# The convolution layer's first product: three 256-column matmuls a weight tile become one of 256 and one of 512, in two banks a column pair

## The chip, the cores and the metric

The kernel runs on one core of one Trainium2 chip. The metric is the device time of one execution in microseconds (us), lower is better; the figure for a kernel is the median of its runs. The core's engines are named as in the profile: PE is TensorE (PEld its weight loads), DVE is VectorE, ACT is ScalarE, POOL is GpSimd, SP is SyncE, which here issues the DMAs.

## The reference, cut to what matters

Four layers on 256 frames of width 1024. Each layer adds a token mixer to the residual and then a squared-ReLU MLP, both behind an RMS norm. The mixers are retention, convolution, stick-breaking attention, retention. The change touches the convolution mixer of the second layer only:

```python
def conformer_conv_mixer(xn, pw1_w, pw1_b, dw_w, dw_b, ln_w, ln_b, pw2_w, pw2_b):
    h = xn @ pw1_w + pw1_b                      # (256, 1024) @ (1024, 2048)
    a, gate = jnp.split(h, 2, axis=-1)
    h = a * jax.nn.sigmoid(gate)
    h = ...   # causal depthwise convolution of h, 31 taps, + dw_b
    h = layer_norm(h, ln_w, ln_b)
    h = jax.nn.silu(h)
    return h @ pw2_w + pw2_b
```

## The kernel before, in words

**Numbers.** All weights are float32. A large product is computed from a rounded high part and a low part (the rest) of each operand, as float32r matmuls: weight high by activation high, weight high by activation low, weight low by activation high. The activations lie transposed, features on partitions: a tile `z` of 128 x 512 holds the 256 columns of the high part of 128 features and, behind them, the 256 columns of the low part.

**Weights.** They come in units of 128 x 1024 (four contraction tiles of 256 output columns), two units in one DMA into a `raw` buffer. For each unit, `unit_hi` lets ACT copy the high part into `wh` (line 354) and `unit_lo` lets DVE subtract it from the raw weights into `wl` (line 361). There are five buffers each of `wh` and `wl`.

**Two ways of a product.** `mm_b` works on one accumulator bank (`acc`, 128 x 512, four of them) that holds a column pair: 256 columns for each of the two weight tiles m. For each weight tile it issues the three matmuls of 256 columns (lines 508, 509, 510), all into the same 256 columns of the bank. `mm_w` works on two banks, one for each weight tile m: one matmul of 256 columns, weight low by activation high, into the first half of the bank (line 524), and one of 512 columns, weight high by both parts of the activation at once, into the whole bank (line 528). The two halves of a bank then still have to be added: `sum_w` lets ACT copy the second half into an SBUF tile (line 571) and DVE add the first half to it (line 572), for each of the two banks. `mm_w` with `sum_w` computes the feed-forward products of most layers; there, too, DVE multiplies the sum by the norm's factor `rb` (line 652).

**The convolution layer (`conv`).** Its first product has 16 units, n = 0 to 15: for each of four column pairs p, two units of the gate's columns (parts 0 and 1, accumulated in `pg`) and two of the value's (parts 2 and 3, in `pa`). The program order of PE and DVE is written out by hand (`manual_schedule`); ACT and POOL follow the order that the scheduler works out with a simulated timeline, and each engine works off its own queue in order. In an iteration n there come, on DVE: the low part of unit n + 3 (`fetch`), then taps of the depthwise convolution for channel tile 0 (`tap_dve`, lines 1010 and 1012), and, where a half ends, the multiplication of the product by `rb` out of the accumulator: `gate_in` (line 969) behind the gate's second unit, with the sigmoid on ACT (line 972), and `glu` (line 977) behind the value's second unit, with the two instructions of line 982 that make the gated tiles `hc` (two channel tiles a pair). For pair 0 the norm's factor is only worked out during unit 1 and broadcast during unit 2 (`norm_r`, `bcast`), so that `gate_in` of pair 0 comes behind unit 2.

The taps of channel tile 1 run beside this: ACT scales the shifted input into one of three `pr` buffers (line 1017) and POOL adds it up (line 1021), three taps an iteration.

The channel tiles 2 to 7 take their taps as matmuls of 32 x 32 blocks on PE (`taps_pe`, line 1092). For these, `spread` writes two gated tiles to DRAM (line 956) and reads them back in another layout (line 959); `pairsum` (POOL, line 992) forms sums of neighbouring columns from it. Behind the first product the order of all four engines is written out by hand: `glu(3)`, `spread(6, 1)` for the last two tiles, `pairsum(2)`, `sum_1`, `pairsum(3)`, the matmul taps of tiles 2 and 3, `shift_a`, `shift_b`, `shift_bb` (a column sum on PE, line 404, its copy on DVE, line 1154, and its broadcast on PE, line 411), the taps of tiles 4 and 5, then of 6 and 7. The accumulators for `taps_pe` come from the same four banks in rotation. Four weight loads of the second product (`unit_raw`, line 369) are issued behind the last DMA of `spread(6, 1)`.

Of the kernel before, what the change touches and what calls it, by code (L numbers as in the profile page):

```python
# [17 lines left out]
S = 256  # L18
# [224 lines left out]
def v3(ap, a, b):  # L243
    return ap.rearrange("p (a b) -> p a b", a=a, b=b)


class Trunk:
# [680 lines left out]
    def conv(self, j, nxt):  # L928
        nc = self.nc
        self.table("sigmoid_and_others")  # L930
        hc = []
        rb = None
# [3 lines left out]
        n = len(PET) * 16  # L936
# [14 lines left out]
        def spread(d0, step):  # L951
            t = self.raw.tile([P, RAWW], F32, name=self.nm("raw"), tag="raw")
            for d in range(d0, d0 + 2, step):
                rows = self.dram.tile([step, 4, 32, HL], F32, name=self.nm("hd"), tag=f"hd{step}")
                for i in range(step):
                    nc.sync.dma_start(rows[i].rearrange("j c u -> (j c) u"), hc[d + i][:, :HL])
                o, n = (d - d0) * 4 * HW, step * 4
                for s in range(4):
                    last = nc.sync.dma_start(
                        v3(t[32 * s : 32 * s + 32, o : o + n * HW], n, HW),  # L960
                        rows.rearrange("i j c u -> c (i j) u")[:, :, NG * s : NG * s + HW],
                    )
                for i in range(step):
                    h4[d + i] = t[:, o + i * 4 * HW : o + (i + 1) * 4 * HW]
            return last

        def gate_in(p, pg):
            u, sg = self.tmp(), self.tmp()
            nc.vector.tensor_mul(v3(u, 2, S), v3(pg, 2, S), self.b2(rb))
            for f in range(2):  # L970
                s = slice(f * S, (f + 1) * S)
                nc.scalar.activation(out=sg[:, s], in_=u[:, s], func=AF.Sigmoid, bias=self.p("pw1b", 8 + 2 * p + f))
            return sg

        def glu(p, pa, sg):
            va = self.tmp()
            nc.vector.tensor_mul(v3(va, 2, S), v3(pa, 2, S), self.b2(rb))
            for f in range(2):
                s = slice(f * S, (f + 1) * S)
                o = self.bigt()  # L980
                nc.gpsimd.memset(o[:, :CW], 0.0)
                nc.vector.scalar_tensor_tensor(
                    out=o[:, CW : CW + S], in0=va[:, s], scalar=self.p("pw1b", 2 * p + f), in1=sg[:, s],
                    op0=ALU.add, op1=ALU.mult,
                )
                hc.append(o)
# [40 lines left out]
        def fetch(n):  # L1027
            if n < len(pw1):
                w[n] = self.unit(("conv_pw1_w", j, "b", pw1[n][1], pw1[n][0]))
# [4 lines left out]
        def taps(n, m):  # L1034
            for k, (tap_, t, r, c) in enumerate(((tap_dve, 0, r0, n), (tap_pool, 1, r1, m))):
                for x in range(at[k], min((CW0, CW)[t], at[k] + c)):
                    tap_(t, x, r[x % 2], x < 2)
                at[k] += c
# [6 lines left out]
        with self.tc.manual_schedule(engines={mybir.EngineType.PE, mybir.EngineType.DVE}):  # L1045
            for n in range(4):
                fetch(n)
            for n in range(16):
                p, part = divmod(n, 4)
                if part == 0:  # L1050
                    pg, pa = self.acc(), self.acc()
                if p:
                    fetch(n + 3)
                    taps((2, 2, 1, 1)[part], 3)
                if n == 13:
                    spread(2, 2)
                if n == 15:
                    spread(4, 2)
                self.mm_b(
                    (pg, pa)[part // 2], w.pop(n), self.zs, part % 2 * 4, part % 2 == 0, part % 2 == 1,  # L1060
                    (lambda kk: self.norm_r(False) if kk == 3 else None) if n == 1 else None,
                )
                if n in (1, 2):
                    fetch(n + 3)
                if n == 2:
                    rb = self.bcast(self.r, "rb")
                    sg = gate_in(0, pg)
                if n == 3:
                    fetch(6)
                if part == 1 and p:  # L1070
                    sg = gate_in(p, pg)
                if part == 3 and p < 3:
                    glu(p, pa, sg)
# [152 lines left out]

        with self.tc.manual_schedule(engines=MANUAL):
            glu(3, pa, sg)
            sp = spread(6, 1)
            with self.tc.issue_after(sp.ins):  # L1230
# [314 lines left out]
```

## Time and profile before

| | |
|---|---|
| median of 3 runs | 1353.01 us (1352.46 to 1353.32) |
| the profiled execution's own time | 1354.99 us |
| its span, first to last instruction | 1353.2 us |
| PE busy | 1340.9 us, 8957 matmuls |
| DVE busy | 987.2 us, 1646 instructions |
| ACT busy | 778.2 us, 1171 instructions |
| POOL busy | 151.9 us, 139 instructions |
| mean granted TensorE clock | 0.997 |

How to read the profile's lines. In a row of the order of time stand the start, the time taken, the engine, the line of the kernel, the operation, the tile written and the tiles read, the sizes, and the count of instructions that the row merges; in brackets the idle time of the engine just before, and what released it. A row of a table of stretches has the stretch and its length, then for each engine the busy time and the count of instructions, then the granted clock as a share of full speed, the share of time in which the DMA engines were busy and what they moved in GB/s. Matmuls overlap, so that the distance between their starts tells the rate, not their durations.

### The profile page before, as it was taken

Reading aid. Unit: us, or ns where it says so; the run is one execution under the profiler, and the core shown is the slowest. Engines: PE = TensorE matmul, PEld = TensorE weight load, DVE = VectorE, ACT = ScalarE, POOL = GpSimd, SP = SyncE. Lnnn points to the kernel's source line nnn. Section 1 sums busy time; section 2 is a strip of 40 time slices with the busy share of each in tenths; the row PEclk is TensorE's granted clock in tenths of the full one; section 3 lists DMA queues with packets and bytes.
Section 4 is the critical chain, followed back from the end, with each engine's and each line's share of the span. In section 5 each row is a group of like instructions: output and inputs, shape, how many; then the busy total and the mean of one; then the engine's idle time right before and its main releaser. Section 6 shows DMA issues by size and latency. Waiting matters only on the chain.

```text
span 1353.2 us, 22237 instructions
## 1 busy us (share of the span) xinstructions
PE 1340.9 (99%) x8957; PEld 1207.9 (89%) x8957; DVE 987.2 (73%) x1646; ACT 778.2 (58%) x1171; POOL 151.9 (11%) x139
## 2 busy tenths in 40 slices
PE   9999999999999999999999999999999999999998
PEld 7989999888899898888878898888888999988886
DVE  6977778875688588765688587755697687788643
ACT  7555556774457367654568667744575555555442
POOL 3201003000169210000100010000120010100000
PEclk9999999999999999999999999999999999999999
DMA  7644445555545645555553345555554444555551
GB/s 283 214 179 152 156 156 192 207 191 188 187 157 145 198 170 204 187 186 187 186 177 126 134 159 188 194 193 196 179 177 180 156 153 160 188 186 187 203 186 62
DMA packets 39287, 240.48 MB, mean 178 GB/s; under 512 B 4368, under 2 KB 8848, under 8 KB 11792
## 3 DMA queue, kind: packets, MB, share of 16 engines
q1 hardware_dynamic: 39040, 238.80, 50.1%
q8 instruction: 70, 1.15, 0.4%
q14 instruction: 33, 0.27, 0.1%
q10 hardware_dynamic: 144, 0.26, 0.1%
HBM read 237.11 MB, written 1.93 MB: 177 GB/s over the span
## 4 chain that ended last, share of the span: by engine, by line
PE 99%; DMA 0%; ACT 0%; DVE 0%; issue 0%; SPq 0%
PE acc L528 30%; PE acc L524 16%; PE acc L508 8%; PE acc L510 8%; PE acc L509 8%; PE acc L687 6%; PE acc L923 4%; PE acc L924 4%; PE acc L925 4%; PE acc L1092 1%; PE acc L1222 1%; PE mis L404 1%; PE mis L819 1%; PE mis L843 1%; PE mis L411 0%; PE mis L1450 0%
## 5 line engine op out<-in xcount | busy, mean ns | idle before, releaser
L361 DVE TENSOR_TENSOR wl<-raw,wh 128x1024 fp32r<-128x1024 f32 (+1 forms) x440 | 547.1, 1248 | 244.0 <-ACT wh L354 237.8
L354 ACT CAST wh<-raw 128x1024 fp32r<-128x1024 f32 (+1 forms) x440 | 456.6, 1041 | 374.5 <-PE acc L528 148.8
L528 PE MATMUL acc<-z,wh 128*128 128x512 f32 x1120 | 387.4, 392 | 0.0
L524 PE MATMUL acc<-z,wl 128*128 128x256 f32 x1120 | 310.5, 281 | 0.0
L528 PEld LDWEIGHTS acc<-z,wh 128*128 128x128 f32 x1120 | 208.3, 187 | 44.6
L528 PE MATMUL acc<-big,wh 128*128 128x512 f32 x672 | 233.1, 391 | 0.0
L524 PEld LDWEIGHTS acc<-z,wl 128*128 128x128 f32 x1120 | 211.1, 189 | 1.7
L524 PE MATMUL acc<-big,wl 128*128 128x256 f32 x672 | 188.2, 280 | 0.0
L528 PEld LDWEIGHTS acc<-big,wh 128*128 128x128 f32 x672 | 125.7, 187 | 27.6
L508 PE MATMUL acc<-z,wh 128*128 128x256 f32 x512 | 145.5, 285 | 0.0
L510 PE MATMUL acc<-z,wl 128*128 128x256 f32 x512 | 145.1, 284 | 0.0
L509 PE MATMUL acc<-z,wh 128*128 128x256 f32 x512 | 144.9, 283 | 0.0
L524 PEld LDWEIGHTS acc<-big,wl 128*128 128x128 f32 x672 | 127.0, 189 | 0.0
L510 PE MATMUL acc<-big,wl 128*128 128x256 f32 x416 | 117.3, 283 | 0.0
L508 PE MATMUL acc<-big,wh 128*128 128x256 f32 x416 | 117.1, 285 | 0.0
L509 PE MATMUL acc<-big,wh 128*128 128x256 f32 x416 | 117.0, 283 | 0.0
L459 POOL TENSOR_TENSOR t<-t,t 128x512 f32<-128x512 f32 x23 | 36.0, 1566 | 682.1 <-ACT t L454 634.0
L571 ACT COPY t<-acc 128x256 f32<-128x256 f32 x164 | 57.7, 372 | 89.4 <-PE acc L528 87.1
L509 PEld LDWEIGHTS acc<-z,wh 128*128 128x128 f32 x512 | 98.1, 192 | 0.0
L508 PEld LDWEIGHTS acc<-z,wh 128*128 128x128 f32 x512 | 98.1, 192 | 0.0
L510 PEld LDWEIGHTS acc<-z,wl 128*128 128x128 f32 x512 | 98.1, 192 | 0.0
L923 PE MATMUL acc<-wh,z 128*128 128x512 f32 x224 | 87.9, 393 | 0.0
(256 smaller groups left out, 2016.0 us busy)
## 6 DMA issues: line engine op xcount, KB each, us to landing
raw<-in_w SPq DMA_DIRECT2D x214, 1024.0 KB, 4.8
raw<-in_w SPq DMA_DIRECT2D x8, 512.0 KB, 8.1
raw<-hd SPq DMA_DIRECT2D x8, 263.0 KB, 4.8
raw<-hd SPq DMA_DIRECT2D x8, 131.5 KB, 3.7
x<-in_x SPq DMA_DIRECT2D x4, 256.0 KB, 6.1
wh<-in_w SPq DMA_DIRECT2D x2, 512.0 KB, 6.1
wl<-in_w SPq DMA_DIRECT2D x2, 512.0 KB, 6.8
hd<-big SPq DMA_DIRECT2D x6, 143.5 KB, 2.3
```

Of the source, the lines that this page charges most:

```text
L354: nc.scalar.copy(hi[:, s], src[:, s])
L361: self.nc.vector.tensor_sub(lo[:, s], src[:, s], hi[:, s])
L508: nc.tensor.matmul(o, wh[:, kk, cs], ah, start=st, stop=False, **kw)
L509: nc.tensor.matmul(o, wh[:, kk, cs], al, start=False, stop=False, **kw)
L510: nc.tensor.matmul(o, wl[:, kk, cs], ah, start=False, stop=en, **kw)
L524: mm = nc.tensor.matmul(ps[m][:, :S], wl[:, kk, cs], a[:, :S], start=first and kk == 0, stop=False, **kw)
L528: nc.tensor.matmul(ps[m], wh[:, kk, cs], a, start=False, stop=last and kk == 3, **kw)
L571: nc.scalar.copy(o[:, s], ps[m][:, S:])
L687: self.tc.keep_in_program_order(nc.tensor.matmul(ps[t], l, r[:, kk], start=False, stop=kb * 2 + kk == 31 and n == 2, **kw))
L923: nc.tensor.matmul(ps[t], zh[:, s], wh[:, kk], start=k == 0, stop=False, skip_group_check=True)
L924: nc.tensor.matmul(ps[t], zh[:, s], wl[:, kk], start=False, stop=False, skip_group_check=True)
L925: nc.tensor.matmul(ps[t], zl[:, s], wh[:, kk], start=False, stop=k == 7, skip_group_check=True)
```

## The change

The gate's and the value's product each get two accumulators for a column pair instead of one, `mm_w` takes the place of `mm_b`, and `sum_w` comes ahead of the multiplication by `rb`, which then works in place on the SBUF tile of the sum. The small norm step inside unit 1 stays at the same place (the fourth contraction tile of that unit: its number is 3 within the unit for `mm_b` and 7 over the product for `mm_w`). Nothing else is edited.

```diff
         def gate_in(p, pg):
-            u, sg = self.tmp(), self.tmp()
-            nc.vector.tensor_mul(v3(u, 2, S), v3(pg, 2, S), self.b2(rb))
+            u, sg = self.sum_w(pg), self.tmp()
+            nc.vector.tensor_mul(v3(u, 2, S), v3(u, 2, S), self.b2(rb))
...
         def glu(p, pa, sg):
-            va = self.tmp()
-            nc.vector.tensor_mul(v3(va, 2, S), v3(pa, 2, S), self.b2(rb))
+            va = self.sum_w(pa)
+            nc.vector.tensor_mul(v3(va, 2, S), v3(va, 2, S), self.b2(rb))
...
                 if part == 0:
-                    pg, pa = self.acc(), self.acc()
+                    pg, pa = (self.acc(), self.acc()), (self.acc(), self.acc())
...
-                self.mm_b(
+                self.mm_w(
                     (pg, pa)[part // 2], w.pop(n), self.zs, part % 2 * 4, part % 2 == 0, part % 2 == 1,
-                    (lambda kk: self.norm_r(False) if kk == 3 else None) if n == 1 else None,
+                    before=(lambda k: self.norm_r(False) if k == 7 else None) if n == 1 else None,
                 )
```

The functions that it calls, as they stand:

```python
    def mm_w(self, ps, w, acts, k0, first, last, keep=False, before=None):
        ...
        for kk in range(4):
            if before is not None:
                before(k0 + kk)
            a = acts(k0 + kk)
            for m in range(2):
                cs = slice(m * P, (m + 1) * P)

                mm = nc.tensor.matmul(ps[m][:, :S], wl[:, kk, cs], a[:, :S], start=first and kk == 0, stop=False, **kw)
                ...
                    nc.tensor.matmul(ps[m], wh[:, kk, cs], a, start=False, stop=last and kk == 3, **kw)

    def sum_w(self, ps):
        nc = self.nc
        o = self.tmp()
        for m in range(2):
            s = slice(m * S, (m + 1) * S)
            nc.scalar.copy(o[:, s], ps[m][:, S:])
            nc.vector.tensor_add(o[:, s], ps[m][:, :S], o[:, s])
        return o
```

## The prediction

> **What bounds the kernel now.** I began with the page's busy times and the chain that ended last, and then went to the stage that the change touches: a table of busy times by stretch, and the order of time of each engine in it.
>
> ```profile
> PE 1340.9 (99%) x8957; PEld 1207.9 (89%) x8957; DVE 987.2 (73%) x1646; ACT 778.2 (58%) x1171; POOL 151.9 (11%) x139
> PE 99%; DMA 0%; ACT 0%; DVE 0%; issue 0%; SPq 0%
> ```
>
> PE (TensorE) is busy for 99% of the span and is 99% of the chain. Any PE time saved counts if nothing else then holds PE up, and any wait put on PE is paid in full, since PE has no later slack. So two questions decide: how much PE time goes, and whether the first product still keeps PE fed.
>
> ```profile
> 390.27 0.28 PE L508 MATMUL acc<-z,wh 128*128 128x256 f32 x1
> 433.95 0.28 PE L510 MATMUL acc<-z,wl 128*128 128x256 f32 x1
> 437.55 0.28 PE L510 MATMUL acc<-z,wl 128*128 128x256 f32 x1
> 349.68 0.39 PE L528 MATMUL acc<-big,wh 128*128 128x512 f32 x1
> 353.50 0.39 PE L528 MATMUL acc<-big,wh 128*128 128x512 f32 x1
> ```
>
> The first and third rows bound the first product: from 390.27 to 437.67 (one step behind the last start), 47.4 us for 16 weight units of 24 matmuls, and some small matmuls of the norm. Starts, not durations, give the rate, since matmuls overlap.
>
> Now the other engines. These three rows are the last three column pairs, p = 1, 2, 3, each from one pair's last gate multiplication to the next one's:
>
> ```profile
> 403.31:414.83 11.52, 11.52 (x98) 11.52 (x97) 10.08 (x15) 9.87 (x18) 8.25 (x8) 1.00 0.57 202
> 414.83:426.35 11.52, 11.52 (x98) 11.52 (x97) 11.26 (x14) 8.50 (x16) 11.52 (x11) 1.00 0.63 148
> 426.35:437.87 11.52, 11.52 (x100) 11.39 (x102) 7.61 (x12) 6.62 (x14) 11.52 (x15) 1.00 0.56 120
> ```
>
> The columns are length, then busy time of PE, weight loads, DVE (VectorE), ACT (ScalarE), POOL (GpSimd). In the middle pair DVE is busy for 11.26 of 11.52 us: there it is as full as PE. POOL is busy all the time, with the additions of the depthwise convolution's second tile. DVE's order is fixed by hand:
>
> ```profile
> 401.57 0.69 DVE L969 TENSOR_TENSOR t<-acc,rb 128x512 f32<-128x512 f32 x1 [1.07 <-ACT rb L417]
> 403.31 0.69 DVE L977 TENSOR_TENSOR t<-acc,rb 128x512 f32<-128x512 f32 x1
> 404.91 1.22 DVE L361 TENSOR_TENSOR wl<-raw,wh 128x1024 fp32r<-128x1024 f32 x1
> 413.10 0.48 DVE L1012 SCALAR_TENSOR_TENSOR mis<-big,prm,mis 128x256 f32<-128x256 f32 x1
> 414.83 0.69 DVE L977 TENSOR_TENSOR t<-acc,rb 128x512 f32<-128x512 f32 x1 [1.26 <-PE acc L510]
> 425.80 0.48 DVE L1012 SCALAR_TENSOR_TENSOR mis<-big,prm,mis 128x256 f32<-128x256 f32 x1
> 426.35 0.69 DVE L977 TENSOR_TENSOR t<-acc,rb 128x512 f32<-128x512 f32 x1
> 428.96 1.76 DVE L361 TENSOR_TENSOR wl<-raw,wh 128x1024 fp32r<-128x1024 f32 x1
> 437.87 0.69 DVE L977 TENSOR_TENSOR t<-acc,rb 128x512 f32<-128x512 f32 x1 [3.67 <-PE acc L510]
> 441.71 0.15 DVE L1154 COPY lns<-mis 128x2 f32<-128x2 f32 x1
> ```
>
> DVE waits for PE 1.26 us ahead of pair 1's value half, nothing ahead of pair 2's (425.80 + 0.48 runs up to 426.35), and 3.67 us ahead of pair 3's. These 4.93 us are all the room that it has.
>
> **The change part by part.**
>
> *PE.* Per weight tile three matmuls of 256 columns become one of 256 and one of 512. Old rate: ten triples between 433.95 and 437.55, 0.360 us each, so 46.1 us for 128 weight tiles; the other 1.3 us are the norm's small matmuls. New rate, from the two-bank form in the feed-forward rows (line 528): eleven pairs between 349.68 and 353.50, 0.347 us each. 128 x 0.0125 = 1.6 us, 0.10 us a unit. That is all that the change can gain here directly. The weight loads fall from three to two a tile; they run beside matmuls.
>
> The Trainium skill ("TensorE: Matmul & The Clock Gate", Part 1, "Wait — 56ns, not 53.3ns?") gives a warm matmul's start-to-start time as its columns over 2.4 GHz plus about 2.5 ns. By that, an estimate, the triple takes 327.5 ns and the pair 325.0 ns, and the gain would be 0.3 us. The rows measure 360 and 347 ns, so I keep 1.6.
>
> *ACT and DVE.* Each of the eight halves (gate and value of four pairs) gets two copies on ACT and two additions on DVE ahead of its multiplication, and the multiplication reads SBUF where it read PSUM. The same helper and the same multiplication stand in the feed-forward part:
>
> ```profile
> 367.10 0.72 ACT L571 COPY t<-acc 128x256 f32<-128x256 f32 x2 [1.37 <-PE acc L528]
> 367.50 0.77 DVE L572 TENSOR_TENSOR t<-acc,t 128x256 f32<-128x256 f32 x2 [0.52 <-ACT t L571]
> 368.31 1.50 DVE L652 TENSOR_TENSOR t<-t,rb 128x512 f32<-128x512 f32 x1
> L652 DVE TENSOR_TENSOR t<-t,rb x9: 691/692/1496, 323.9 to 945.0; 128x512 f32<-128x512 f32 x9
> L361 DVE TENSOR_TENSOR wl<-raw,wh 128x1024 fp32r<-128x1024 f32 x10 | 15.0, 1498 | 0.0
> ```
>
> The additions take 0.80 us of DVE a half (367.50 to 368.31). The multiplication from SBUF takes 0.69 us at best and 1.50 at worst. In this stage the other two-SBUF-input instruction, the low-part subtraction of line 361, averages 1.498 us (last row: the ten from 403.31 to 437.87) against 1.22 at 404.91, before POOL starts: +0.28. I take +0.27 a multiplication, between 0 and +0.80.
>
> The Trainium skill ("SBUF — State Buffer", "SBUF: two separate sides") says that a VectorE instruction with two SBUF inputs and a GpSimd one that reads SBUF exclude each other for a whole instruction. This speaks against the change. Its worst case would be about one POOL addition on each multiplication, as the 1.50 us row shows at its extreme; the +0.28 is the mean that this stage shows.
>
> The additions also wait for the copies, and ACT's order is first come, first served:
>
> ```profile
> 419.35 0.51 ACT L1017 ACTIVATE pr<-big,prm 128x256 f32<-128x256 f32 x1 [1.17 <-POOL big L1021]
> 421.94 0.68 DVE L969 TENSOR_TENSOR t<-acc,rb 128x512 f32<-128x512 f32 x1
> 425.24 0.89 ACT L972 ACTIVATE t<-t,prm 128x256 f32<-128x256 f32 x2
> ```
>
> ACT's tap scalings wait for POOL (up to 1.17 us), and what stands behind them waits too: pair 2's sigmoid ran at 425.24 though its input was ready at 422.62. A copy so placed holds up DVE, and behind it every subtraction and tap. I take 0.15 us a half, between 0 and 1.17.
>
> So a half costs DVE 0.80 + 0.27 + 0.15 = 1.22 us more. The first gate half has DVE waiting for rb (1.07 us) and costs nothing; the first value half, with POOL not yet running, 0.80. DVE's delay then runs: 0.8; pair 1's gate 2.0; the 1.26 us of room leaves 0.8, its value half 2.0; pair 2: 3.2, 4.4; pair 3's gate 5.6; the 3.67 us of room leaves 2.0; its value half 3.2. With waits and contention at nothing the last figure is +0.7, with 1.50 us multiplications and 0.5 us of waiting +8.5.
>
> *Buffers.* Each pair now takes all four accumulators, so a half must be summed before the next pair writes its banks two units (5.5 us) later: enough up to a delay of about 4 us. Late subtractions bite sooner: pair 3's last one ends at 430.72 (428.96 + 1.76), and 4.4 us later is 435.1, where the last unit wants it at about 433.3 (437.67 less 2.88, less 15 x 0.10). PE would wait some 2 us there. That costs nothing extra, because of what follows.
>
> *What waits for the last half.*
>
> ```profile
> 440.68 0.61 PE L404 MATMUL mis<-cst,big 128*128 128x1 f32 x4
> 442.23 0.71 PE L411 MATMUL mis<-cst,lns 128*128 128x128 f32 x4
> 447.58 1.06 POOL L992 TENSOR_TENSOR t<-raw 128x524 f32<-128x524 f32 x1 [1.42 <-DMA raw<-hd]
> 447.66 1.14 PE L1092 MATMUL acc<-raw,big 128*32 128x128 f32 x32
> 454.50 2.95 PE L1092 MATMUL acc<-raw,big 128*32 128x128 f32 x50 [2.03 <-issue]
> 454.50:458.00 3.50, 3.50 (x62) 3.22 (x64) 0.29 (x1) 0.31 (x1) 0.00 (x0) 0.51 0.26 48
> ```
>
> The last half's product goes to DRAM and back (spread), and tile 6's taps use it. POOL was waiting for that DMA until 447.58, and PE began those taps at 447.66: no slack. In between, PE's broadcast at 442.23 waits for DVE's copy at 441.71, behind the last half in DVE's order, with 0.4 us of slack. So PE begins tile 6 as late as the last half ends: 3.2 us less the 0.1 of slack, where without the delay it would come 1.6 us early. Nothing behind gives it back.
>
> *The sum:* +3.1 us on the profiled span of 1353.2. The profiled execution's own time is 1354.99 (1.8 around its span), 2.0 above the median of the runs, 1353.01; I add the difference to the median: 1353.0 + 3.1, rounded to 1356.0.
>
> Two more losses stand in the last two rows: 2.03 us in which PE waited for nothing that the profile shows, and then a granted clock of 0.51 for 3.5 us, so about 1.7 us lost. I leave both: the same instructions come at the same place behind the same DMAs.
>
> **The rivals.**
>
> *PE stays the bound* and the 1.6 us stand: 1351.4, not slower. For it: the room of 4.93 us, and ACT's and DVE's means of 8.33 and 9.65 of 11.52 us over the three pairs. Against it: pair 2 has no room. It decides where the delay of the last half falls under about -1.5, which even the lowest bound (+0.7) does not reach, unless the scheduler places work so that DVE's waits shrink.
>
> *The broken supply to the taps disappears:* if PE comes to tile 6 later than its DMAs do, the 2.03 us and the half clock go: 1353.0 - 1.6 - 2.0 - 1.7 = 1347.7. For it: the stall follows a crowd of DMAs. Against it: these DMAs are issued behind the same late half.
>
> *A second stretch of half clock.* If PE's new waits between 433 and 445 bring another one, it costs up to 1.7 us: 1356.0 + 1.7 = 1357.7. For it: the one in the trace follows a PE wait of 2.03 us, and my waits are as long. Against it: part of it would fall into time in which PE waits anyway.
>
> The Trainium skill ("TensorE: Matmul & The Clock Gate", "What's actually happening") says that the half clock comes after an idle window of about 3.4 us. The trace has it behind 2.03 us, so that a wait shorter than the window is no protection here.
>
> **How the numbers follow.** A time within 0.2% (2.7 us) is about what a measurement of this kernel cannot tell from no change. The DVE delay has 0.60: likeliest 1356.0, its own range 1353.7 to 1359.5; some 0.22 of it lies within 2.7 us of before, 0.38 above. PE staying the bound has 0.20, within. The second half clock has 0.13, slower. The vanished stall has 0.07, faster. Together 0.07 faster, 0.42 same, 0.51 slower. The range 1350.8 to 1360.0 leaves out the vanished stall and the tail toward +8.5.
>
> **What would show it.** In the changed trace: the first product's weight tiles at 0.347 us where PE does not wait; two copies and two additions a half, 16 of each more; the multiplications of lines 969 and 977 reading SBUF, above 0.9 us on average; DVE without an idle gap ahead of pair 1's and pair 2's value halves; PE waiting for a low part in the last unit or for a bank at the first taps; tile 6's taps starting about 3 us later than 447.66. If DVE still waits for PE ahead of pair 3's value half, the forecast is wrong toward faster; if the additions wait long for the copies, toward slower.

## The result, and the profile after

The changed kernel took 1355.76 us (median of 22 runs, 1354.42 to 1357.78) against 1353.95 us for the kernel before, timed beside it (22 runs, 1352.16 to 1354.94): a ratio of 1.0016, 95% interval 1.0010 to 1.0022. It is slower by about 2 us (1.8 by the medians, 2.2 by the ratio); forecast were 3.0, at 1356.0. That the time lies so close to 1356.0 is in part luck: the kernel before had a median 0.94 us above the 1353.01 us from which the forecast counted. The profiled execution took 1355.67 us, with a span of 1353.9 us.

The page of the kernel after, busy times and the chain that ended last:

```profile
PE 1339.2 (99%) x8829; PEld 1200.2 (89%) x8829; DVE 995.4 (74%) x1662; ACT 782.2 (58%) x1187; POOL 157.2 (12%) x139
PE 95%; DVE 2%; DMA 1%; ACT 1%; issue 0%; POOL 0%; SPq 0%; POOLq 0%; ACTq 0%
```

There are 128 matmuls fewer and 16 instructions more on each of DVE and ACT, as the change says. The chain that lay on PE for 99% of the span now lies on it for 95%. Where it leaves PE is seen in the chain in order of time (start, length, engine, tile, line), kernel after:

```profile
412.81 1.73 POOL big L1021
414.57 0.51 ACT pr L1017
415.37 0.77 DVE t L572 x2
416.16 1.03 DVE t L977
...
444.01 0.71 PE mis L411 x4
```

From the middle of the first product to the broadcast the chain runs mostly through DVE, and ahead of that through tap scalings on ACT and tap additions on POOL. PE's order of time in the kernel after, from the first product to the taps of tiles 6 and 7, with the first row of the feed-forward part last:

```profile
389.55 0.28 PE L524 MATMUL acc<-z,wl 128*128 128x256 f32 x1
...
434.34 0.39 PE L524 MATMUL acc<-z,wl 128*128 128x256 f32 x1 [1.06 <-DVE wl L361]
434.57 0.40 PE L528 MATMUL acc<-z,wh 128*128 128x512 f32 x1
...
437.00 0.39 PE L528 MATMUL acc<-z,wh 128*128 128x512 f32 x1
...
444.01 0.71 PE L411 MATMUL mis<-cst,lns 128*128 128x128 f32 x4 [1.90 <-DVE lns L1154]
444.65 4.55 PE L1092 MATMUL acc<-raw,big 128*32 128x128 f32 x96
...
450.76 1.13 PE L1092 MATMUL acc<-raw,big 128*32 128x128 f32 x32
...
456.69 1.70 PE L1092 MATMUL acc<-raw,big 128*32 128x128 f32 x50 [1.24 <-issue]
...
492.42 0.40 PE L524 MATMUL acc<-z,wl 128*128 128x256 f32 x2
```

And two rows of the same view of the kernel before:

```profile
442.87 3.01 PE L1092 MATMUL acc<-raw,big 128*32 128x128 f32 x96
491.75 0.40 PE L524 MATMUL acc<-z,wl 128*128 128x256 f32 x2
```

The two executions differ by 0.72 us already ahead of the product (390.27 against 389.55), which is not the change. So I count every start from the product's first matmul, here and in all that follows, and call four of them marks: the product's last matmul, the broadcast (line 411), the first taps of tile 6, and the feed-forward part's first matmul. Behind the last mark the two executions run equally long (about 861.4 us to the end), so it holds all that the change did.

| mark | before | after | difference |
|---|---|---|---|
| product's last matmul | 47.28 | 47.45 | +0.17 |
| broadcast | 51.96 | 54.46 | +2.50 |
| tile 6 | 57.39 | 61.21 | +3.82 |
| feed-forward | 101.48 | 102.87 | +1.39 |

PE's faster matmuls do not bring the product's end forward, since PE has to wait for DVE in the last units, 1.06 us of it in one wait for a late low part. The broadcast waits 1.90 us for DVE, and tile 6 comes 3.82 us later. Behind tile 6, 2.43 us come back, and two things give them: the wait for "issue" is 1.24 instead of 2.03 us, and the half clock has moved. Two stretches of the kernel after:

```profile
445.30:448.80 3.50, 3.50 (x78) 3.50 (x71) 3.12 (x9) 2.86 (x5) 3.27 (x5) 0.51 1.01 229
455.00:458.50 3.50, 2.26 (x75) 1.96 (x67) 1.19 (x4) 0.60 (x2) 0.00 (x0) 1.00 0.37 145
```

The granted clock is 0.51 from 445.3, ahead of tile 6, and 1.00 where it was 0.51 before. The 96 taps at 444.65 take 4.55 us for 3.01. Only about half of that seems to be lost: without a stretch at half clock (late_new, below) the changed kernel waits 0.52 us ahead of tile 6 and begins it 0.76 us earlier.

DVE's order of time in the stage, kernel after, and one row of POOL's:

```profile
403.24 0.69 DVE L977 TENSOR_TENSOR t<-t,rb 128x512 f32<-128x512 f32 x1
...
415.37 0.76 DVE L572 TENSOR_TENSOR t<-acc,t 128x256 f32<-128x256 f32 x2 [1.03 <-ACT t L571]
416.16 1.02 DVE L977 TENSOR_TENSOR t<-t,rb 128x512 f32<-128x512 f32 x1
...
430.09 0.75 DVE L977 TENSOR_TENSOR t<-t,rb 128x512 f32<-128x512 f32 x1
...
436.96 1.26 DVE L969 TENSOR_TENSOR t<-t,rb 128x512 f32<-128x512 f32 x1
...
439.46 0.76 DVE L572 TENSOR_TENSOR t<-acc,t 128x256 f32<-128x256 f32 x2 [0.31 <-ACT t L571]
440.25 1.28 DVE L977 TENSOR_TENSOR t<-t,rb 128x512 f32<-128x512 f32 x1
441.56 0.88 DVE L982 SCALAR_TENSOR_TENSOR big<-t,prm,t 128x256 f32<-128x256 f32 x2
...
443.80 0.15 DVE L1154 COPY lns<-mis 128x2 f32<-128x2 f32 x1
```

```profile
439.91 1.06 POOL L992 TENSOR_TENSOR t<-raw 128x524 f32<-128x524 f32 x1
```

DVE's waits for PE ahead of the halves (1.26 and 3.67 us) are gone. In their place stand two waits for copies. The last multiplication, 1.28 us long, began while POOL's row was running and ended 0.56 us behind that row's end. The groups of the stretch from 396 to 442 us in the kernel after (count, busy time, mean ns of one, idle time before):

```profile
L969 DVE TENSOR_TENSOR t<-t,rb 128x512 f32<-128x512 f32 x4 | 3.8, 952 | 0.3 <-ACT rb L417 0.2
L977 DVE TENSOR_TENSOR t<-t,rb 128x512 f32<-128x512 f32 x4 | 3.7, 935 | 0.1
```

### The profile page after: what moved, and what is told of

It is laid out like the page before. It is cut to its first block, busy times and chain, and to the rows that moved or that the text cites. A ratio compares the mean times of both kernels' runs of the same rounds, so it can differ in the third digit from the quotient of the medians.

```text
span 1353.9 us, 22008 instructions
## 1 busy us (share of the span) xinstructions
PE 1339.2 (99%) x8829; PEld 1200.2 (89%) x8829; DVE 995.4 (74%) x1662; ACT 782.2 (58%) x1187; POOL 157.2 (12%) x139
## 4 chain that ended last, share of the span: by engine, by line
PE 95%; DVE 2%; DMA 1%; ACT 1%; issue 0%; POOL 0%; SPq 0%; POOLq 0%; ACTq 0%
PE acc L528 31%; PE acc L524 16%; PE acc L510 7%; PE acc L508 7%; PE acc L509 7%; PE acc L687 6%; PE acc L923 4%; PE acc L924 4%; PE acc L925 4%; PE acc L1222 1%; PE acc L1092 1%; DMA raw<-in_w 1%; DVE wl L361 1%; PE mis L404 1%; PE mis L819 1%; PE mis L843 1%
## 5 line engine op out<-in xcount | busy, mean ns | idle before, releaser
L528 PE MATMUL acc<-z,wh 128*128 128x512 f32 x1248 | 432.4, 392 | 0.0
L528 PEld LDWEIGHTS acc<-z,wh 128*128 128x128 f32 x1248 | 232.3, 187 | 49.8
L524 PEld LDWEIGHTS acc<-z,wl 128*128 128x128 f32 x1248 | 235.3, 189 | 3.5 <-DVE wl L361 1.6
L571 ACT COPY t<-acc 128x256 f32<-128x256 f32 x180 | 62.9, 371 | 87.6 <-PE acc L528 87.3
L508 PE MATMUL acc<-z,wh 128*128 128x256 f32 x384 | 109.1, 285 | 0.0
L509 PE MATMUL acc<-z,wh 128*128 128x256 f32 x384 | 108.7, 284 | 0.0
L572 DVE TENSOR_TENSOR t<-acc,t 128x256 f32<-128x256 f32 x180 | 70.5, 421 | 29.4 <-ACT t L571 29.1
L923 PE MATMUL acc<-wh,z 128*128 128x512 f32 x224 | 87.9, 393 | 0.0
L924 PE MATMUL acc<-wl,z 128*128 128x512 f32 x224 | 87.5, 391 | 0.0
L925 PE MATMUL acc<-wh,z 128*128 128x512 f32 x224 | 87.4, 390 | 0.0
```

The source lines that it names most:

```text
L508: nc.tensor.matmul(o, wh[:, kk, cs], ah, start=st, stop=False, **kw)
L509: nc.tensor.matmul(o, wh[:, kk, cs], al, start=False, stop=False, **kw)
L524: mm = nc.tensor.matmul(ps[m][:, :S], wl[:, kk, cs], a[:, :S], start=first and kk == 0, stop=False, **kw)
L528: nc.tensor.matmul(ps[m], wh[:, kk, cs], a, start=False, stop=last and kk == 3, **kw)
L572: nc.vector.tensor_add(o[:, s], ps[m][:, :S], o[:, s])
L923: nc.tensor.matmul(ps[t], zh[:, s], wh[:, kk], start=k == 0, stop=False, skip_group_check=True)
```

## The experiments

All were timed beside the kernel before on the same chip. The marks, the stall and the half clock are those of the one profiled execution of each kernel; that of act_free_new, 1355.38 us, was the longest of its 11. "Stall" is the longest time in which PE waited for "issue" in the taps, "half" the time at half clock between the product's first matmul and the feed-forward's.

| kernel | ratio (95%) | product | broadcast | tile 6 | feed-forward | stall | half |
|---|---|---|---|---|---|---|---|
| before | 1 | 47.28 | 51.96 | 57.39 | 101.48 | 2.03 | 3.4 |
| after | 1.0016 (1.0010 to 1.0022) | 47.45 | 54.46 | 61.21 | 102.87 | 1.24 | 3.4 |
| no_sum | 0.9988 (0.9979 to 0.9997) | 45.65 | 50.40 | 55.63 | 98.45 | 2.28 | 0 |
| sum_only | 1.0082 (1.0068 to 1.0096) | 56.73 | 63.70 | 71.38 | 112.77 | 1.00 | 10.2 |
| relief_new | 1.0014 (1.0005 to 1.0022) | 47.44 | 53.94 | 59.65 | 103.01 | 2.78 | 0 |
| relief_old | 0.9998 (0.9989 to 1.0007) | 47.28 | 52.53 | 57.74 | 100.17 | 1.84 | 0 |
| act_free_new | 1.0000 (0.9992 to 1.0009) | 45.65 | 52.49 | 57.71 | 102.33 | 2.70 | 3.4 |
| relief_act_free_new | 0.9992 (0.9983 to 1.0001) | 45.65 | 51.81 | 57.03 | 99.72 | 1.59 | 0 |
| room | 1.0011 (1.0002 to 1.0020) | 46.95 | 51.92 | 57.14 | 103.13 | 2.45 | 6.8 |
| late_old | 0.9979 (0.9970 to 0.9988) | 47.28 | 51.96 | 57.57 | 97.75 | 0 | 0 |
| late_new | 1.0012 (1.0004 to 1.0021) | 47.46 | 54.46 | 60.45 | 100.85 | 0 | 0 |
| late_no_sum | 0.9970 (0.9958 to 0.9982) | 45.65 | 50.40 | 55.86 | 96.05 | 0 | 0 |
| late_last_old | 1.0000 (0.9991 to 1.0008) | 47.41 | 53.54 | 59.41 | 99.91 | 0 | 0 |
| late_room | 0.9988 (0.9979 to 0.9996) | 46.95 | 51.92 | 58.86 | 99.07 | 0 | 0 |

**The matmuls alone: no_sum.** The changed kernel with the halves not added.

```diff
-            u, sg = self.sum_w(pg), self.tmp()
-            nc.vector.tensor_mul(v3(u, 2, S), v3(u, 2, S), self.b2(rb))
+            u, sg = self.tmp(), self.tmp()
+            for m in range(2):
+                nc.vector.tensor_mul(u[:, m * S : (m + 1) * S], pg[m][:, :S], rb)
...   # the same for the value half
```

> The changed kernel with the sums left out: DVE multiplies the first half of each bank by rb straight from the accumulator (two instructions of 256 columns), so weight high by activation low is computed on PE but not added in. No copies on ACT, no additions on DVE, no SBUF to SBUF multiplication. All marks are counted from the product's first matmul; before: last product matmul 47.3 us, broadcast on PE 52.0, first taps of tile 6 57.4, first matmul of the feed-forward 101.5; changed kernel: 47.5, 54.5, 61.2, 102.9. Theory (DVE's additional work delays the last half): DVE has about 0.1 us more a half, so PE's gain of 1.6 us stands: last matmul near 45.7, broadcast 50.5 to 51, tile 6 near 56, feed-forward near 100, ratio to before 0.999. Rival (the two-bank matmuls or their banks cost the time): marks as in the changed kernel, ratio 1.001 or more.

First and last matmul of the product in no_sum:

```profile
389.13 0.28 PE L524 MATMUL acc<-z,wl 128*128 128x256 f32 x1
...
434.78 0.39 PE L528 MATMUL acc<-z,wh 128*128 128x512 f32 x1
```

The last start is at 45.65, 1.63 us earlier than before, and PE waits nowhere in the product. So the new matmul form does save what it should, with the same four accumulators, and copies, additions and SBUF multiplications take it back. Up to 32.0 us behind the first matmul the kernel after has the same unit starts as no_sum; all of the 1.80 us between their last product matmuls are lost in the last five units.

**The additions alone: sum_only.** The old matmuls, with copies and additions out of the one bank.

```diff
+        def sum_1b(ps):
+            o = self.tmp()
+            for m in range(2):
+                s = slice(m * S, (m + 1) * S)
+                nc.scalar.copy(o[:, s], ps[:, s])
+                nc.vector.tensor_add(o[:, s], ps[:, s], o[:, s])
+            return o
...   # for sum_w in both halves; mm_b and one bank a half as before
```

> The kernel before (three matmuls of 256 columns, one bank) with the sums' work put in: for each half two copies on ACT, two additions on DVE of 256 columns, and the multiplication from SBUF in place; the product comes out doubled by this. Theory (DVE's additional work): last product matmul at 47.3 us or up to 1 us later, DVE's last half 2.5 to 3.2 us late, broadcast near 54.5, tile 6 near 60.5 to 61, feed-forward 102 to 103.5, ratio 1.001 to 1.002. Rival (the two banks): broadcast 52.0, tile 6 57.4, feed-forward 101.5, ratio 1.000.

The two copies of pair 0's value half, the first addition and what stands between, ACT and DVE in order of time, sum_only:

```profile
403.58 0.35 ACT L971 COPY t<-acc 128x256 f32<-128x256 f32 x1
403.96 0.43 DVE L972 TENSOR_TENSOR t<-acc,t 128x256 f32<-128x256 f32 x1 [1.54 <-ACT t L971]
404.70 1.05 ACT L354 CAST wh<-raw 128x1024 fp32r<-128x1024 f32 x1 [0.77 <-PE acc L509]
405.66 0.36 ACT L971 COPY t<-acc 128x256 f32<-128x256 f32 x1
```

This was a poor control, and it missed its expectation at every mark. The second copy starts 1.27 us behind the first addition's end, where the changed kernel's copies, and its additions, follow each other. In this half the copy of a weight unit's high part (line 354) stands between the two in ACT's queue, and it waits 0.77 us for PE itself; in later halves tap scalings stand there. Where nothing stands between, at pair 3's gate half, ACT was idle for 7.13 us ahead of the second copy and began it 0.03 us behind the first addition: there the copy waits for the addition. Why it has to was not settled. DVE waits ten times for copies, 11.8 us in all, and the product ends 9.45 us late. It doesn't price the additions of the change. It does show how dear a copy is that comes late to a DVE that works in order.

**Is it DVE's work, or the order on ACT?** In relief_new 16 of the 25 taps of tile 0 are left out on DVE, which gives it back about what the change took (16 taps of 0.48 us, against eight times 0.79 + 0.25); relief_old is the kernel before with the same cut. In act_free_new ACT's scalings of tile 1's taps are left out after the first two (POOL adds the unscaled input), so that the copies have ACT nearly to themselves. relief_act_free_new has both cuts.

```diff
-                    tap_(t, x, r[x % 2], x < 2)
+                    if k or not 2 <= x < 18:
+                        tap_(t, x, r[x % 2], x < 2)      # relief
...
+            if t == 1 and not first:
+                nc.gpsimd.tensor_add(a, a, tap(t, w))    # act_free
+                return
```

> The changed kernel with 16 of DVE's 25 taps of tile 0 left out (those of pairs 1 to 3), about 8 us of DVE time. To be compared with relief_old. Theory (DVE's additional work): with DVE freed only the last half's own latency is left, two additions and a slower multiplication, 0.8 to 1.4 us, against 1.6 us of PE gain: no PE wait in the last unit, last matmul near 45.7, broadcast within 0.5 us of relief_old, tile 6 too, so the two kernels within 1 us of each other. Rival (copies queued on ACT, or banks): relief_new stays later than relief_old by 2 us or more at the broadcast.

> The kernel before with the same 16 taps of tile 0 left out. DVE had room at the end of pairs 1 and 3 and none at pair 2, and PE never waited for it: the marks stay at 47.3, 52.0 (or up to 0.4 earlier), 57.4 and 101.5, ratio 1.000. If the marks come clearly earlier, DVE held PE up already before the change.

> The changed kernel with 29 of the 31 tap scalings of tile 1 left out on ACT: POOL adds the unscaled shifted input instead, as often as before. ACT's copies then stand behind nothing that waits for POOL. DVE keeps all its taps. Theory A (DVE's additional work, two additions and a slower multiplication a half): only DVE's waits for copies go, 1.3 us in the changed kernel; broadcast about 53 us behind the product's first matmul (changed kernel 54.5, before 52.0), tile 6 at 59.5 to 60, ratio to before about 1.001. Theory B (copies queued on ACT behind scalings that POOL paces): the whole delay goes, broadcast at 52 or earlier, tile 6 at 57.4 or earlier, ratio 1.000 or below.

> The changed kernel with both left out: 16 of DVE's 25 taps of tile 0 and 29 of ACT's 31 scalings of tile 1. If DVE's work and ACT's order together are the whole cause, PE's gain shows: no wait for a low part in the last unit, last product matmul near 45.7 us, broadcast within 0.5 us of relief_old (52.5) or earlier, tile 6 near 56.5. If the four accumulators or something else hold it up, the last matmul stays near 47.4 and DVE or PE shows a wait that is neither a copy nor a low part.

My theory, DVE's work, failed in relief_new: the broadcast came only 0.52 us earlier than in the kernel after, and 1.41 us later than in relief_old, which is neither my theory's 0.5 us nor the rival's 2. The expectation for relief_old failed too: its broadcast came 0.57 us later than before, not at 52.0 or earlier. But the broadcast is not a clean mark of the last half. Behind the last multiplication DVE makes the two gated tiles (line 982), and these two instructions took 0.88 us in the kernel after; in the kernel before and in relief_new:

```profile
438.66 1.69 DVE L982 SCALAR_TENSOR_TENSOR big<-t,prm,t 128x256 f32<-128x256 f32 x2
```

```profile
439.45 2.16 DVE L982 SCALAR_TENSOR_TENSOR big<-t,prm,t 128x256 f32<-128x256 f32 x2
```

In pair 0, before POOL starts, they take 0.87 or 0.88 us in every kernel here, and in the kernel after POOL was idle when each of the last two began. So the last half is better judged where its multiplication ends:

| kernel | last multiplication ends | gated tiles take | broadcast |
|---|---|---|---|
| before | 48.29 | 1.69 | 51.96 |
| after | 51.98 | 0.88 | 54.46 |
| relief_new | 50.17 | 2.16 | 53.94 |
| relief_old | 48.29 | 2.57 | 52.53 |
| act_free_new | 48.74 | 2.16 | 52.49 |
| relief_act_free_new | 47.63 | 2.16 | 51.81 |

There relief_new gets 1.81 of the 3.69 us back, all of it behind pair 2, whose value half ends at 41.29 us as in the kernel after. The waits from 389 to 452 us in the kernel after, then those from 388 to 452 us in relief_new (total, times, longest):

```profile
ACT pr L1017 <- POOL big L1021: 6.8, 11, 1.2
...
DVE t L572 <- ACT t L571: 1.3, 2, 1.0
```


```profile
DVE t L572 <- ACT t L571: 5.8, 5, 1.4
PE acc L524 <- DVE wl L361: 1.5, 1, 1.5
```

DVE's waits for copies had grown from 1.3 to 5.8 us: most of what it no longer worked, it waited. The copies stand in ACT's queue among tap scalings, and these wait for POOL 11 times. The same view of act_free_new, and its DVE groups from 396 to 441 us:

```profile
DVE t L572 <- ACT t L571: 0.3, 1, 0.3
```

```profile
L969 DVE TENSOR_TENSOR t<-t,rb 128x512 f32<-128x512 f32 x4 | 3.3, 832 | 0.3 <-ACT rb L417 0.2
L977 DVE TENSOR_TENSOR t<-t,rb 128x512 f32<-128x512 f32 x4 | 2.8, 705 | 0.1
```

With ACT free, the waits are down to 0.3 us, the product ends as early as in no_sum, and 3.24 of the 3.69 us go at the last multiplication, 1.97 of the 2.50 at the broadcast; the multiplications are faster too, 0.77 us for 0.94 on average. But DVE's full load still leaves the broadcast 2.1 us behind no_sum's. With both cuts the broadcast is at 51.81 and the feed-forward at 99.72, no later than in relief_old (100.17, with a 0.25 us longer stall). So two things make the delay, DVE's own work and copies queued on ACT behind tap scalings that POOL paces, and with only one of them taken away the other still holds a part. Freeing ACT gave back more, but the shares are not shown: the faster multiplications alone are worth 1.4 us over the eight halves, and there is no run of the kernel before with ACT's scalings left out.

**The wide form only where DVE had room: room.** Gate halves of pairs 0, 1 and 3 in the new form, the other five in the old one.

```diff
-                    pg, pa = (self.acc(), self.acc()), (self.acc(), self.acc())
+                    pg, pa = (
+                        (self.acc(), self.acc()) if (p, h) in [(0, 0), (1, 0), (3, 0)] else self.acc() for h in range(2)
+                    )
...   # mm_w with sum_w for a tuple, mm_b without it otherwise
```

> The new form only for three halves, the gate halves of pairs 0, 1 and 3, where DVE had room before (waiting for rb, 1.26 us, 3.67 us); the five others in the old form. Theory A: no delay of the last half, PE's gain 3 x 0.2 = 0.6 us: last product matmul near 46.7 us, broadcast 51.4 to 52.0, tile 6 56.8 to 57.4, ratio 0.9995 (below what can be told). Theory B: the copies delay DVE at these halves too, by up to 1.2 us each, of which pair 3's room takes most: broadcast up to 52.5, ratio 1.000 to 1.001.

Up to tile 6 all came about as planned: the last product matmul at 46.95, the broadcast no later than before (51.92). DVE did wait 2.2 us for copies at pair 3's gate half, and the room there took it. Then, in PE's order of time and the table of stretches of room:

```profile
455.31 0.34 PE L1102 MATMUL acc<-raw,big 128*32 128x128 f32 x4 [2.45 <-issue]
```

```profile
456.90:463.70 6.80, 6.80 (x96) 5.19 (x99) 3.99 (x22) 2.12 (x7) 0.00 (x0) 0.50 0.52 172
```

A longer stall and 6.8 us at half clock ate it. What happens in the taps varies by as much as what was to be measured.

**Taking the stall away: the late kernels.** Four weight loads of the second product (2 MB) are issued behind the end of `spread`, while the taps run. In late_old, the kernel before, they are issued only behind pairsum(7), which a memset of one column by POOL holds to its place.

```diff
-            with self.tc.issue_after(sp.ins):
-
-                W = [self.unit_raw(key(0, p), ("wh", "wl")[p % 2]) for p in range(4)]
...
             taps_pe(7, 0)
+            with self.tc.issue_after(sp.ins):
+                W = [self.unit_raw(key(0, p), ("wh", "wl")[p % 2], True) for p in range(4)]
...   # in unit_raw
+        if late:
+            self.nc.gpsimd.memset(t[:, :1], 0.0)
```

> The kernel before with the four weight loads of the second product issued later, behind a small POOL memset that follows pairsum(7) (in the old marks at about 60.5 us instead of 56.6). The trace of before has 2.03 us in which PE waits for nothing shown, while these loads and the last reads of the spread fill the DMA engines. Theory (these loads hold up PE's supply of instructions): the wait falls below 0.7 us, the feed-forward's first matmul comes at 98 to 100 us instead of 101.5, ratio 0.997 to 0.999. Rival (the stall has another cause, or the spread's own reads suffice): the wait stays near 2 us, ratio 1.000; or the later loads make the second product wait and it is slower.

PE in order of time, late_old:

```profile
388.81 0.28 PE L510 MATMUL acc<-z,wh 128*128 128x256 f32 x1
...
446.38 1.18 PE L1094 MATMUL acc<-raw,big 128*32 128x128 f32 x32 [0.21 <-DVE big L1177]
...
450.97 1.52 PE L1094 MATMUL acc<-raw,big 128*32 128x128 f32 x44
...
486.56 0.40 PE L526 MATMUL acc<-z,wl 128*128 128x256 f32 x2
```

There is neither stall nor half clock, and the feed-forward starts 3.73 us earlier, which is what the 2.03 us and the about 1.7 us of the half clock make together. With a median of 1350.07 us against 1353.07, ratio 0.9979 (0.9970 to 0.9988), this version is faster than both kernels. It also gives a ground on which the change can be weighed without the stall: late_new is the changed kernel with the same late loads, late_no_sum has no_sum's halves besides, late_last_old has the last value half alone in the old form, late_room is room with late loads.

> The changed kernel with the four weight loads of the second product issued later, as in late_old. Marks of late_old, from the product's first matmul: last product matmul 47.3 us, broadcast 52.0, first taps of tile 6 57.6, first matmul of the feed-forward 97.8, no wait for nothing shown; ratio to before 0.9979. Theory (the delay of the last half is carried to the end, and in the changed kernel's profile a shorter stall hid part of it): broadcast 54.4, tile 6 at 60 to 61, feed-forward at 100.3 to 100.8 (up to 102.3 if half a clock follows the wait at the broadcast), no stall above 0.5 us, ratio to before 0.9995 to 1.001, so about 0.2% slower than late_old. Rival (work behind tile 6 gives the delay back): feed-forward within 1 us of 97.8, ratio 0.998.

> no_sum (the changed kernel without sums: the second half of each bank is not added in) with the four weight loads later. With no stall left and no additional work on DVE, the difference to late_old is PE's gain alone: last product matmul 45.7 us, broadcast 50.4, feed-forward at 96.1 to 96.4 against 97.8, ratio to before 0.9965 to 0.997. If it is not 1.3 to 1.7 us ahead of late_old, the gain of the two-bank form is lost behind the product whatever the sums cost.

> late_new with the last value half (pair 3) alone back in the old form, so that it has no copies, additions or SBUF multiplication of its own; the seven other halves stay new. Theory (DVE's accumulated delay plus the last half's own work): the last half's own 1.2 to 1.7 us go, the delay accumulated before stays: broadcast 52.8 to 53.3, feed-forward 98.6 to 99.3. Rival (only the last half's latency counts, what came before is absorbed by pair 3's room): broadcast 52.0 or earlier, feed-forward at 97.8 or earlier. Second rival (only what was accumulated counts): unchanged against late_new.

> room (new form for the gate halves of pairs 0, 1 and 3 only) with the four weight loads later. In room the marks up to tile 6 were those of before or earlier and the time was lost in a stall of 2.4 us and 6.8 us of half clock behind them. If that is so, without the stall the feed-forward's first matmul comes at 97.4 to 97.8 us, as in late_old or 0.3 earlier, ratio to before 0.9975 to 0.998. If room's loss came from the new form, it stays 1 us or more behind late_old.

PE in order of time, late_new, and the feed-forward's first row in late_no_sum:

```profile
389.61 0.28 PE L526 MATMUL acc<-z,wl 128*128 128x256 f32 x1
...
444.07 0.71 PE L413 MATMUL mis<-cst,lns 128*128 128x128 f32 x4 [1.89 <-DVE lns L1156]
...
450.06 1.13 PE L1094 MATMUL acc<-raw,big 128*32 128x128 f32 x32 [0.52 <-DVE big L1177]
...
490.46 0.40 PE L526 MATMUL acc<-z,wl 128*128 128x256 f32 x2
```

```profile
485.33 0.40 PE L526 MATMUL acc<-z,wl 128*128 128x256 f32 x2
```

On this ground the change costs 100.85 - 97.75 = 3.10 us, and the matmuls alone gain 97.75 - 96.05 = 1.70. The ratios, 1.0012 and 0.9979 from two chips, lie 4.5 us apart, by their intervals between 2.2 and 6.9. The marks leave one loss out: 8 of late_new's 12 runs have a mean granted clock of 0.998 or less, none of late_old's 11, and every profiled execution here with so low a clock has a stretch of half clock in this table, while those at 0.999 or more have none. The profiled execution of late_new is one of the latter. late_last_old shows where the delay is made. Its feed-forward is 0.94 us earlier than late_new's, and 2.16 of the 3.10 us stay; I had expected more of the last half itself. At the end of the last multiplication, though, 1.80 of the 3.69 us are gone (50.18 against 51.98): there the last half and the ones ahead of it have about equal parts. Its gated tiles then take 1.69 us for 0.88, and that gives 0.81 us back.

late_room's feed-forward is 4.06 us ahead of room's, the cost of stall and half clock, but it is 1.32 behind late_old's, which the expectation had named as the sign of a loss by the new form. POOL's row in late_room:

```profile
447.83 1.06 POOL L1002 TENSOR_TENSOR t<-raw 128x524 f32<-128x524 f32 x1 [2.84 <-DMA raw<-hd]
```

POOL waits 2.84 us for the data of `spread` and tile 6 comes at 58.86, 1.29 later than in late_old. The first read is issued 0.52 us later (52.73 against 52.21), and the rest arises on the way through DRAM; whether that is chance or belongs to the mixed form stays open.

## Why the prediction was right, and the step that was off

- *PE gains 1.6 us.* Right: 1.63 us at the product's end in no_sum, 1.70 at the feed-forward in late_no_sum. In the kernel after, seven steps between 434.57 and 437.00 take 0.347 us each.
- *A half costs DVE 0.80 + 0.27 + 0.15.* The additions took 0.79 us (415.37 to 416.16). The multiplications averaged 0.94 us against 0.69, so +0.25. The waits for copies were 1.34 us over eight halves, 0.17 each. The mean hides a spread: 0.69 us before POOL starts, 1.26 and 1.28 in the last pair. What sets it is seen in the rows: the two multiplications ahead of POOL's start took 0.69 us, and each of the other six ended 0.55 or 0.56 us behind the end of a POOL instruction that was running when it began. This agrees with the rule of the Trainium skill ("SBUF — State Buffer", "SBUF: two separate sides") that the two exclude each other for a whole instruction. So what is added is the rest of the POOL instruction that a multiplication meets, and the mean that was forecast was a good size for eight of them, but not for the single last one.
- *The delay adds up and the room absorbs it.* From the ends of the multiplications of line 977, after against before: 0.65, 2.38, 4.52 and 3.69 us for the four value halves; forecast 0.8, 2.0, 4.4 and 3.2. Pair 3's gate half was 5.66 us late, and the 3.67 us of room brought it to about 2. One sign came otherwise: ahead of pair 1's value half DVE did have an idle gap, 1.03 us, now for copies.
- *PE waits about 2 us for a low part.* 1.06 us in one wait; the rest of the 1.80 us by which its last product matmul lags no_sum's was lost in smaller pieces from 32.0 us on. It cost nothing extra, as forecast: the broadcast, DVE's copy behind it and tile 6 are set by DVE's last half.
- *Tile 6 starts 3.1 us later.* 2.88 us in late_new over late_old (60.45 against 57.57); 3.82 in the kernel after, where tile 6 came 0.76 us behind late_new's, with the half clock ahead of it. That 3.1 was so near is in part luck: the last multiplication ended 3.69 us late for the 3.2 forecast, and the gated tiles, which the sum left out, gave 0.81 us back because POOL was idle when they began.
- *"I leave both" (stall and half clock).* This is the step that was off. They did not stay: the stall became 0.79 us shorter, and the half clock moved ahead of tile 6, where half of its price was hidden. Of the 3.82 us, 2.43 came back, and +1.39 was left in this execution and about 2 in the runs. With both taken away, late_new over late_old is +3.10 us: the sum that was forecast, +3.1, for the change itself, with the luck just named. The vanished-stall rival had the right mechanism in part: the stall does depend on when transfers meet the taps, and it shrank without vanishing.
- *The rivals.* PE as the bound fails with the vanished waits of DVE for PE and the 1.90 us at the broadcast. Of the second stretch of half clock, one stretch only is in the trace, but it came where that rival said, behind the new wait of PE at the broadcast; the old one behind the stall did not come.

What the forecast did not see is that its two terms, DVE's work and the copies' wait, are not a sum from which one can be struck: relief_new took away about as much work as the change had added and got 1.81 of the 3.69 us back at the last multiplication, 0.52 of the 2.50 at the broadcast.

## What to carry to other kernels

A faster matmul form pays only where the engine that finishes its output has room in that very stage: find the waits of that engine for PE, add up what each half costs it, and carry the delay along until room absorbs it. If a helper needs a second engine whose queue is paced by a third, price the wait beside the work, for with one gone the other can still hold the result. And where a trace shows PE waiting for nothing while transfers crowd in, issue the transfers that are not yet needed later: that was worth more here (3 us) than the matmul form (1.7 us).

## What the runs showed of the hardware that was not expected

- PE's wait for "issue" in the dense small matmuls, 1.00 to 2.78 us in every kernel with the early loads, is gone in all five with the late ones. That the loads cause it is shown; through what, is not.
- The half clock does not follow the length of PE's wait. After 1.90 us (after) it came, after 1.89 us (late_new's profiled execution) not; after a stall of 2.03 us (before) it came, after 2.28 and 2.78 (no_sum, relief_new) not; in room it lasted 6.8 us. Of the 27 runs of the kernel before that stand beside no_sum, the 12 with a mean granted clock of 0.998 or less have a median of 1354.67 us, the other 15 one of 1352.64. So about 2 us between two single executions of this kernel can go with the clock alone, which is as much as the change itself; where the half clock lay in the runs without a trace is not known.
- How long a DVE instruction with two SBUF inputs took was set by the POOL instruction that it met. Of the eight multiplications in the kernel after two took 0.69 us without POOL; the six beside it took 0.75 to 1.28 us, and each ended 0.55 or 0.56 us behind a POOL instruction's end. The last two instructions of line 982 together varied from 0.88 us (POOL idle when they began, kernel after) to 2.57 (relief_old), and each one that was lengthened ended 0.28 or 0.29 us behind a POOL instruction's end. That is a difference of 1.69 us at the broadcast, which the change moved by 2.50.
